# Early output projection by column halves over four tiles, in a two-layer encoder kernel

## The chip, the cores and the metric

The kernel runs on one core of one Trainium2 chip. The metric is the device time of the whole program in microseconds; the time before is the median of three runs. The profile shows one further execution.

## The reference

A two-layer encoder trunk over 1024 tokens of width 1024, all in float32. Each layer normalises its input, projects it with one wide matrix into several head groups and a gate, runs attention in the groups, multiplies the concatenated heads by SiLU(gate) and applies an output projection that is added to the residual. Cut to what matters here:

```python
def even_layer(x, mem_n, ...):                     # layer 0
    h = rmsnorm(x, norm_g)
    aq, ak, av, bq, bk, bv, xq, gate = _split(h @ w_in, EVEN_SPLITS)
    y_a = windowed_gqa_sink(...)                   # (A) 6 heads, band of 128
    y_b = dense_gqa_blocked(...)                   # (B) 6 heads, dense
    y_x = memory_cross_attention(xq, mem_n, ...)   # (X) 4 heads, 256 memory tokens
    y = concat([y_a, y_b, y_x]) * silu(gate)       # (1024, 1024)
    return x + y @ w_out

def odd_layer(x, mem_n, ...):                      # layer 1
    ...                                            # (C) 6 differential heads, and (X)
    y = concat([y_c, y_x]) * silu(gate)            # (1024, 1024)
    return x + y @ w_out

h = odd_layer(even_layer(x))
return rmsnorm(h, final_norm)
```

## The kernel before

**Products in three matmuls.** Each float32 operand is split into a high part, rounded to the matmul's format, and a low part, the rest. A product is high x high, high x low and low x high, so each 128 x 128 x 512 block of a product is three matmuls. Splitting is a cast on ScalarE (ACT) and a subtraction on VectorE (DVE) or GpSimd (POOL).

**Attention in steps with filling.** `run_steps` (L431) writes down the program of a layer's attention step by step. A step holds one block of 128 queries of a head (in group A 256 queries): scores and exponential (`s1`), a copy of the probabilities through a DMA (`word_copy` or `hop`, tile er), two or three steps later their transposes and splits (`s2`), then the product with v and the gating (`s3`). Layer 0 has 8 steps of X, 8 of the first B head and 64 of B and A mixed, numbered 0 to 79; layer 1 has 8 of X and 48 of C, 0 to 55. After the last step the loop runs four times more for the delayed parts.

Between the parts of a step the loop pulls work that does not depend on it, the filling. It comes from a list of jobs (`Jobs`, L88): first the input projections (`proj_jobs`, L277: 24 matmuls for 512 tokens of a 128-wide piece, tile acc), then the early output projection. One pull is eight matmuls, and `fill` says how many a step pulls, half of them ahead of the rest of the step and half at its end: 3 a step in X, in the first B head and in all of C, 1 in the rest of layer 0. A job whose condition is not met holds up those behind it in the list. The tile framework then places the program's instructions on the engines' queues, each of which runs in order, so in the trace pulled matmuls appear mixed with the attention's. All DMAs named here are issued by one queue, SyncE's (SP).

**The early output projection.** The concatenated, gated heads are stored in DRAM (`ysc`) as eight rows m of 128 channels, in the order in which they are finished (`KORD`); `stored` says which are there. `pre_job` (L645) takes one tile of 128 tokens, loads its first `EARLY[l]` rows (`y_chunk`, L613: DMAs into tile yr, then a split into yh and yl), and for each of the two column halves of the output multiplies them by w_out (`y_mm`, L632, tile pre), adds the residual (tile xh) and stores the sum in DRAM (`xpsc`). This is done for tiles 2 to 7 with five rows in layer 0 and for tiles 2 and 3 with seven rows in layer 1 (`PRE`, L42).

```python
when=lambda: len(wout) == 16 and all((l, m) in stored for m in range(EARLY[l]))
```

**w_out.** `load_wout` (L246) brings w_out in sixteen pieces of 128 x 512: pieces 0 to 7 are the rows of the first column half, 8 to 15 those of the second. The raw piece (tile wor) lands in a buffer of the wr kind (two) for the first half and of the wr, wh and wl kinds (two, four, four; the same as the weights and the y chunks use) for the second, is cast by ACT (woh), and its rest is taken by DVE for even pieces and POOL for odd ones (wol). The split pieces take the place of the layer's input hT, whose first half of tokens is free when the last projection job has come to its second half (`half`), and the second when that job is done. `wout_hook` (L258) is called once a step and issues up to `WRATE[l]` pieces, 3 in layer 0 and 4 in layer 1.

**The rest of the output projection.** `out_proj` (L1173) goes through the eight tiles in the order `ORD`. The first two begin with the rows below `EARLY[l]`, while the attention ends; then each tile gets the rows that are still missing (tile po), the residual or the stored partial sum, and the norm. In layer 0 the normalised tile is transposed into the input of layer 1 (`transpose_tile`).

Of the kernel before, what the change touches and what calls it, by code (L numbers as in the profile page):

```python
# [12 lines left out]
F32 = mybir.dt.float32  # L13
# [16 lines left out]
EARLY = (5, 7)  # L30
# [7 lines left out]
WRATE = (3, 4)  # L38
# [3 lines left out]
PRE = (range(2, 8), range(2, 4))  # L42
# [45 lines left out]
class Jobs:  # L88
# [25 lines left out]
    def _advance(self):  # L114
        if self.cur is None:
            i = self._next()
            if i is None:
                return False
            self._load(i)
            self.cur = (i, self.jobs[i]["run"](self.loaded[i]))  # L120
            self._load(i + 1)
        i, gen = self.cur
        try:
            next(gen)
        except StopIteration:
            self.done.update((self.jobs[i]["tag"],) + self.jobs[i].get("also", ()))
            self.loaded[i] = None
            self.cur = None
            return self._advance()
        return True  # L130

# [20 lines left out]
def encoder_kernel(ctx, tc, A):  # L152
# [93 lines left out]
    def load_wout(l, i, pl):  # L246
        nh, k = divmod(i, 8)
        if k == 0:
            wtile.append([pl.tile([P, 8, 512], F32R, tag="h", name="wo" + c, bufs=4) for c in "hl"])
        tag, bufs = (("wr", 2), ("wh", 4), ("wl", 4))[(0, 1, 2, 1, 2)[i % 5] if nh else 0]  # L250
        raw = wp.tile([P, 512], F32, tag=tag, name="wor", bufs=bufs)
        dma(raw, w_out[l][KORD[l][k], :, nh * 512:(nh + 1) * 512])
        hi, lo = (t[:, k, :] for t in wtile[nh])
        (nc.vector.tensor_copy if WHI[l] else nc.scalar.copy)(hi, raw)
        (nc.gpsimd if i % 2 else nc.vector).tensor_tensor(out=lo, in0=raw, in1=hi, op=ALU.subtract)
        return hi, lo

    def wout_hook(l, jobs, last, pl):  # L258
        lim = 16 if last in jobs.done else 8 if half[0] else 0
        for _ in range(WRATE[l]):  # L260
            if len(wout) < lim:
                wout[len(wout)] = load_wout(l, len(wout), pl)

    wout, wtile, half = {}, [], [False]

    def half_done():
        half[0] = True
# [9 lines left out]
    def proj_jobs(ws, hT, ntok, consumes, on_half=None):  # L277
        hh, hl = hT
        pend = []
        for c0, wi in ((c0, wi) for c0 in range(0, ntok, 512) for wi in range(len(ws))):  # L280
            if c0 > 0 and wi == 0 and on_half is not None:
                on_half()
# [148 lines left out]
    def run_steps(steps, jobs, hooks=None):  # L431
# [4 lines left out]
        for i in range(n + LAG + 1):  # L436
# [11 lines left out]
            if jobs is not None:  # L448
                jobs.pull(f - f // 2)
            for q in list(posts):  # L450
                q.pop(0)()
                if not q:
                    posts.remove(q)
# [14 lines left out]
            if jobs is not None:  # L468
                jobs.pull(f // 2)
        while posts:  # L470
            for q in list(posts):
                q.pop(0)()
                if not q:
                    posts.remove(q)
# [138 lines left out]
    def y_chunk(l, t, ks):  # L613
        ysv = ysc[l].rearrange("m p (t c) -> t p m c", c=P)
        out = {}
        for kh in range(2):
            for a, b in ((0, EARLY[l]), (EARLY[l], 8)):
# [3 lines left out]
                if (kh, 0) not in out:  # L621
                    out[kh, 0] = (wp.tile([P, 4, P], F32, tag="wr", name="yr", bufs=2),
                                  wp.tile([P, 4, P], F32R, tag="wh", name="yh", bufs=4),
                                  wp.tile([P, 4, P], F32R, tag="wl", name="yl", bufs=4))
                raw, hi, lo = out[kh, 0]
# [3 lines left out]
        return [(out[k // 4, 0][1][:, k % 4, :], out[k // 4, 0][2][:, k % 4, :]) if (k // 4, 0) in out else None  # L629
# [15 lines left out]
    def pre_job(l, t, src):  # L645
        rows = slice(t * P, (t + 1) * P)

        def run(ch):
            pend = []
            i = 0  # L650
            for nh in range(2):
# [4 lines left out]
                for k in range(EARLY[l]):  # L656
                    for _ in y_mm(acc, ch, nh, k, k == 0, k == EARLY[l] - 1):
                        i += 1
                        if i % 8 == 0:
                            yield  # L660
                nc.vector.tensor_tensor(out=xh, in0=acc, in1=xh, op=ALU.add)
                dma(xpsc[l][rows, cols], xh)
        return dict(tag="pre%d" % t, run=run, load=lambda: y_chunk(l, t, range(EARLY[l])),
                    when=lambda: len(wout) == 16 and all((l, m) in stored for m in range(EARLY[l])))

# [241 lines left out]
    for t in PRE[0]:  # L907
        jl.append(pre_job(0, t, x_d))
# [253 lines left out]
    def hooks0(i):  # L1162
        if 2 <= i < 8:
            skew(i - 2)
        wout_hook(0, jobs, "g2", r1)

    run_steps(steps, jobs, hooks0)
# [5 lines left out]
    def out_proj(l, hT_next, stack):  # L1173
# [6 lines left out]
        pre = [t for t in PRE[l] if "pre%d" % t in jobs.done]  # L1180
# [21 lines left out]
        def chunk(t):  # L1202
            return y_chunk(l, t, range(ne if t in pre else 0, 8))
# [5 lines left out]
        for i in range(2):  # L1209
            t = order[i]  # L1210
            accs[i] = pieces(i)
            if t not in pre:
                mm(accs[i][0], chs[i], range(ne), 0)
        xrs = [xres(t) for t in order[:2]]
        for i, t in enumerate(order):
            xr = xrs[i]
            mps, eps = accs[i] if i < 2 else pieces(i)
            mm(mps, chs[i], range(ne if i < 2 or t in pre else 0, 8), ne if t in pre else 0)
# [52 lines left out]
    half[0] = False  # L1271
# [69 lines left out]
    for t in PRE[1]:  # L1341
        jl.append(pre_job(1, t, x1sc))
# [119 lines left out]
    def hooks1(i):  # L1462
        wout_hook(1, jobs, "g5", r2)

    run_steps(steps, jobs, hooks1)
# [76 lines left out]
```

## Time and profile before

| | |
|---|---|
| median of 3 runs | 1274.36 us (1273.86 to 1276.91) |
| the profiled execution | 1277.62 us, span 1275.8 us |
| mean granted clock of TensorE | 0.986 |
| PE busy | 1218.1 us, 95% of the span |
| DVE, ACT, POOL busy | 850.7, 602.9, 426.6 us |
| matmuls of the early part (tile pre) | 264, started between 441.8 and 1190.4 us |

The times of the trace count from the start of the span. PE is TensorE's matmuls, PEld its weight loads, which run beside them. PEclk is the clock that TensorE was granted, as a part of full speed; a matmul at half the clock takes twice as long and counts as busy for that time, so a stretch can be full and still lose time. A row of the waits gives the waiting engine, tile and line, what ended the wait, the sum in us, the number of times and the longest.

### The profile page before, as it was taken

Reading aid. Unit: us, or ns where it says so; the run is one execution under the profiler, and the core shown is the slowest. Engines: PE = TensorE matmul, PEld = TensorE weight load, DVE = VectorE, ACT = ScalarE, POOL = GpSimd, SP = SyncE. Lnnn points to the kernel's source line nnn. Section 1 sums busy time; section 2 is a strip of 40 time slices with the busy share of each in tenths; the row PEclk is TensorE's granted clock in tenths of the full one; section 3 lists DMA queues with packets and bytes.
Section 4 is the critical chain, followed back from the end, with each engine's and each line's share of the span. In section 5 each row is a group of like instructions: output and inputs, shape, how many; then the busy total and the mean of one; then the engine's idle time right before and its main releaser. Section 6 shows DMA issues by size and latency. Waiting matters only on the chain.

```text
span 1275.8 us, 19602 instructions
## 1 busy us (share of the span) xinstructions
PE 1218.1 (95%) x6806; PEld 1008.8 (79%) x6806; DVE 850.7 (67%) x1623; ACT 602.9 (47%) x1275; POOL 426.6 (33%) x390
## 2 busy tenths in 40 slices
PE   6989989999999889999999999999999999999998
PEld 5878878888888678877888788787787877877886
DVE  5567676377778877748367866766767667577444
ACT  6245455266667755634134643444444444464222
POOL 5024255366666644413122212232222322231100
PEclk9999999999999889999999999999999999997999
DMA  6655334545465555467644424242332423353263
GB/s 248 195 183 162 123 146 156 176 157 203 149 223 199 201 191 192 164 184 244 192 138 149 149 91 131 83 139 100 133 121 83 140 99 129 119 199 125 89 215 117
DMA packets 95646, 198.85 MB, mean 156 GB/s; under 512 B 11286, under 2 KB 30998, under 8 KB 95548
## 3 DMA queue, kind: packets, MB, share of 16 engines
q1 hardware_dynamic: 95548, 197.60, 46.5%
q8 instruction: 54, 0.88, 0.3%
q14 instruction: 44, 0.36, 0.1%
HBM read 78.80 MB, written 30.95 MB: 86 GB/s over the span
## 4 chain that ended last, share of the span: by engine, by line
PE 46%; DVE 3%; issue 1%; ACT 1%; DMA 1%; POOL 0%; POOLq 0%; SPq 0%; DVEq 0%; ACTq 0%
PE acc L291 24%; PE po L636 5%; PE oc L1422 5%; PE sc L1383 3%; PE te L517 2%; PE sc L1389 2%; PE pre L636 2%; PE ox L593 1%; PE ssqc L1437 1%; DMA wor<-in_w_out 1%; PE tv L395 1%; PE sx L486 1%; DVE e L1407 1%; DVE mr L1405 0%; ACT e L568 0%
## 5 line engine op out<-in xcount | busy, mean ns | idle before, releaser
L291 PE MATMUL acc<-h,wh 128*128 128x512 f32 x1536 | 498.7, 399 | 5.7 <-DVE wh L235 2.1
L291 PEld LDWEIGHTS acc<-h,wh 128*128 128x128 f32 x1536 | 285.2, 189 | 73.7 <-issue 11.6
L291 PE MATMUL acc<-h,wl 128*128 128x512 f32 x768 | 304.8, 397 | 2.0 <-POOL wl L237 2.0
L237 POOL TENSOR_TENSOR wl<-wr,wh 128x512 fp32r<-128x512 f32 x96 | 124.2, 1295 | 334.4 <-DVE wh L235 132.8
L306 DVE TENSOR_TENSOR PTl<-te,PTh 128x512 fp32r<-128x512 f32 x224 | 146.4, 685 | 68.4 <-ACT PTh L305 67.5
L291 PEld LDWEIGHTS acc<-h,wl 128*128 128x128 f32 x768 | 145.0, 189 | 35.2 <-issue 4.4
L1398 ACT ACTIVATE e<-e,mn 128x1024 f32<-128x1024 f32 x96 | 110.2, 1150 | 111.4 <-DVE mn L1395 111.4
L305 ACT CAST PTh<-te 128x512 fp32r<-128x512 f32 x224 | 123.4, 592 | 64.2 <-PE te L517 56.1
L1395 DVE CUSTOM_DVE_ANT_0 e<-sc,toep 128x1024 f32<-128x1024 f32 x96 | 114.1, 1220 | 20.8 <-PE sc L1389 20.8
L1026 POOL TENSOR_TENSOR e<-e,rz 128x1024 f32<-128x1024 f32 x48 | 92.3, 1926 | 82.3 <-DVE rz L1025 62.7
L517 PEld LDWEIGHTS te<-identr,er 128*128 128x128 f32 x896 | 90.9, 143 | 14.7 <-issue 3.5
L517 PE MATMUL te<-identr,er 128*128 128x128 f32 x896 | 97.9, 247 | 4.0 <-issue 1.7
L1022 ACT ACTIVATE e<-sb,mr,nrq 128x1024 f32<-128x1024 f32 x48 | 58.0, 1209 | 48.6 <-DVE mr L1021 27.9
L235 DVE CAST wh<-wr 128x512 fp32r<-128x512 f32 x112 | 55.5, 498 | 30.9 <-PE acc L291 8.9
L1422 PE MATMUL oc<-PTh,v 128*128 128x256 f32 x384 | 74.9, 288 | 0.0
L636 PE MATMUL po<-woh,yh 128*128 128x512 f32 (+1 forms) x176 | 67.9, 387 | 0.1
L1454 POOL TENSOR_TENSOR gy<-O,gy 128x256 f32<-128x256 f32 x24 | 31.1, 1297 | 108.9 <-DVE O L1451 83.1
L636 PE MATMUL po<-woh,yl 128*128 128x512 f32 (+1 forms) x176 | 67.3, 382 | 0.0
L636 PE MATMUL po<-wol,yh 128*128 128x512 f32 (+1 forms) x176 | 67.2, 382 | 0.0
L1407 DVE SCALAR_TENSOR_TENSOR e<-e,mr 128x1024 f32<-128x1024 f32 x48 | 62.5, 1303 | 1.1
L1422 PEld LDWEIGHTS oc<-PTh,v 128*128 128x128 f32 x384 | 61.4, 191 | 0.7 <-ACT PTh L305 0.6
L1017 DVE TENSOR_REDUCE mn<-sb 128x1 f32<-128x1024 f32 x48 | 58.4, 1216 | 5.0 <-PE sb L486 4.9
(199 smaller groups left out, 2270.7 us busy)
## 6 DMA issues: line engine op xcount, KB each, us to landing
er<-e SPq DMA_DIRECT2D x112, 512.0 KB, 2.9
wr<-in_w_in SPq DMA_DIRECT2D x96, 256.0 KB, 2.7
ysc<-gy SPq DMA_DIRECT2D x16, 512.0 KB, 2.9
wor<-in_w_out SPq DMA_DIRECT2D x32, 256.0 KB, 3.5
cq<-sg SPq DMA_DIRECT2D x64, 128.0 KB, 2.4
ck<-sg SPq DMA_DIRECT2D x48, 128.0 KB, 2.3
er<-e SPq DMA_DIRECT2D x12, 384.0 KB, 3.0
xt<-in_x SPq DMA_DIRECT2D x8, 512.0 KB, 6.0
```

The lines of the kernel that those rows point to most:

```text
L237: (nc.vector if fast else nc.gpsimd).tensor_tensor(out=lo, in0=raw, in1=hi, op=ALU.subtract)
L291: lastmm[0] = nc.tensor.matmul(acc, a, b[:, k, c0:c0 + n], start=(i == 0), stop=(i == 23))
L305: nc.scalar.copy(hi, src)
L306: return nc.vector.tensor_tensor(out=lo, in0=src, in1=hi, op=ALU.subtract)
L517: nc.tensor.transpose(to[:, i * P:(i + 1) * P], e[0][:, k * P:(k + 1) * P], idt)
L636: lastmm[0] = nc.tensor.matmul(acc, a, b, start=(start and n == 0), stop=(stop and n == 2))
L1017: nc.vector.tensor_reduce(out=mn, in_=Sp, op=ALU.min, axis=AX.X)
L1026: nc.gpsimd.tensor_tensor(out=et, in0=et, in1=rz.to_broadcast([P, 1024]), op=ALU.mult)
L1395: nc.vector.tensor_tensor_reduce(out=et, in0=Sp, in1=toeps[h][:, w0:w0 + 1024], scale=1.0, scalar=BIG, op0=ALU.add, op1=ALU.min, accum_out ...
L1398: nc.scalar.activation(et, et, AF.Exp, bias=mn[:, m:m + 1], scale=-1.0, accum_out=z[:, m:m + 1])
L1407: nc.vector.scalar_tensor_tensor(out=es[0], in0=es[1], scalar=c, in1=es[0], op0=ALU.mult, op1=ALU.add)
L1422: nc.tensor.matmul(acc, V[:, kt, v, :], pt[:, kt, :], start=(n == 0), stop=(n == 23))
```

## The change

- **Jobs.** The early part is now a list of groups with their number of rows. Layer 0: tiles 2, 3, 4 and 5 with four rows, tile 6 with six, tile 7 with six. Layer 1: tiles 2 and 3 with six, tile 4 with six. A group of several tiles is two jobs, one for each column half over all its tiles; a single tile stays one job for both halves.
- **Conditions.** A job of the first half asks for eight w_out pieces and the group's rows; the others for sixteen.
- **Chunks.** The chunks of y are loaded one ahead of their use and kept over both halves; the first two are asked for while the last projection job is still running (`half` is 2 then). `CUTS` says where a chunk's loads are divided, so that each part can be loaded by itself.
- **w_out.** The hook that issues the pieces is called after each of the two portions of a step's filling, with 1 piece in layer 0 and 2 in layer 1. Odd pieces land in a buffer of the sg kind (three in layer 0, five in layer 1, also used by xh), even ones in wr.
- **Pace.** Once all projections are done and eight pieces are issued, the filling of a step is set by `pace`: in layer 0 one pull in three steps of four, none in the fourth, in layer 1 two.
- **out_proj** takes for each tile the rows that its early part left out. Tiles 0 and 1 begin with six rows in layer 0 (before: five) and seven in layer 1.

```diff
-EARLY = (5, 7)
+EARLY = (6, 7)
+CUTS = ((0, 4, 6, 8), (0, 4, 6, 7, 8))
-WRATE = (3, 4)
+WRATE = (1, 2)
-PRE = (range(2, 8), range(2, 4))
+PRE = ((((2, 3, 4, 5), 4), ((6,), 6), ((7,), 6)), (((2, 3), 6), ((4,), 6)))
...
+    def projected(self):
+        return all("load" in j or j["tag"] in self.done for j in self.jobs)
...
-        tag, bufs = (("wr", 2), ("wh", 4), ("wl", 4))[(0, 1, 2, 1, 2)[i % 5] if nh else 0]
-        raw = wp.tile([P, 512], F32, tag=tag, name="wor", bufs=bufs)
+        raw = sg(M, "wor", F32) if i % 2 else wp.tile([P, 512], F32, tag="wr", name="wor", bufs=2)
...
     def wout_hook(l, jobs, last, pl):
         lim = 16 if last in jobs.done else 8 if half[0] else 0
+        if half[0] == 2 and len(wout) >= 8 and len(chunks) < 2:
+            pre_chunk(l, len(chunks))
         for _ in range(WRATE[l]):
...
-            if c0 > 0 and wi == 0 and on_half is not None:
-                on_half()
+            if c0 > 0 and on_half is not None:
+                on_half(wi + 1)
...
-    def run_steps(steps, jobs, hooks=None):
+    def run_steps(steps, jobs, hooks=None, pace=None):
...
             if jobs is not None:
+                if half[0] and len(wout) >= 8 and jobs.projected():
+                    f = pace(i)
                 jobs.pull(f - f // 2)
+                if hooks:
+                    hooks(-1)
...
                 jobs.pull(f // 2)
+                if hooks:
+                    hooks(-1)
...
-            for a, b in ((0, EARLY[l]), (EARLY[l], 8)):
+            for a, b in zip(CUTS[l], CUTS[l][1:]):
...
+    def pre_chunk(l, n):
+        order = [(t, k) for ts, k in PRE[l] for t in ts]
+        if n < len(order):
+            t, k = order[n]
+            if t not in chunks and all((l, m) in stored for m in range(k)):
+                chunks[t] = y_chunk(l, t, range(k))
+
+    def pre_jobs(l, src):
+        out = []
+        for ts, k in PRE[l]:
+            parts = [(0,), (1,)] if len(ts) > 1 else [(0, 1)]
+            for nhs in parts:
+                out.append(dict(
+                    tag="pre%s%d" % (ts[0], nhs[0]), also=tuple("pre%d" % t for t in ts) if nhs[-1] else (),
+                    run=lambda _, ts=ts, k=k, nhs=nhs: pre_run(l, ts, k, nhs, src), load=lambda: None,
+                    when=lambda k=k, nhs=nhs: len(wout) >= 8 * nhs[-1] + 8 and all((l, m) in stored for m in range(k))))
+        return out
+
+    def pre_run(l, ts, kn, nhs, src):
+        order = [t for tt, _ in PRE[l] for t in tt]
+        i = 0
+        for nh in nhs:
+            for t in ts:
+                n = order.index(t)
+                pre_chunk(l, n)
...
                 acc = ps_a("pre")
-                for k in range(EARLY[l]):
-                    for _ in y_mm(acc, ch, nh, k, k == 0, k == EARLY[l] - 1):
+                for k in range(kn):
+                    for _ in y_mm(acc, chunks[t], nh, k, k == 0, k == kn - 1):
                         i += 1
                         if i % 8 == 0:
                             yield
+                    if k == 0 and (t != ts[-1] if nh == 0 else t == ts[-1]):
+                        pre_chunk(l, n + 1)
...
     def hooks0(i):
         if 2 <= i < 8:
             skew(i - 2)
-        wout_hook(0, jobs, "g2", r1)
-
-    run_steps(steps, jobs, hooks0)
+        if i < 0:
+            wout_hook(0, jobs, "g2", r1)
+
+    run_steps(steps, jobs, hooks0, lambda i: i % 4 != 3)
...
-        pre = [t for t in PRE[l] if "pre%d" % t in jobs.done]
+        pre = {t: k for ts, k in PRE[l] for t in ts if "pre%d" % t in jobs.done}
...
-            return y_chunk(l, t, range(ne if t in pre else 0, 8))
+            return y_chunk(l, t, range(pre.get(t, 0), 8))
...
-            if t not in pre:
-                mm(accs[i][0], chs[i], range(ne), 0)
+            mm(accs[i][0], chs[i], range(pre.get(t, 0), ne), pre.get(t, 0))
...
-            mm(mps, chs[i], range(ne if i < 2 or t in pre else 0, 8), ne if t in pre else 0)
+            mm(mps, chs[i], range(ne if i < 2 else pre.get(t, 0), 8), pre.get(t, 0))
...
     def hooks1(i):
-        wout_hook(1, jobs, "g5", r2)
-
-    run_steps(steps, jobs, hooks1)
+        if i < 0:
+            wout_hook(1, jobs, "g5", r2)
+
+    run_steps(steps, jobs, hooks1, lambda i: 2)
```

More of the change, by code (lines that the diff above doesn't have):

```diff
@@ L262, in wout_hook, with half_done @@
                 wout[len(wout)] = load_wout(l, len(wout), pl)
-    wout, wtile, half = {}, [], [False]
-    def half_done():
-        half[0] = True
+    wout, wtile, half = {}, [], [0]
+    chunks = {}
+    def half_done(n=1):
+        half[0] = n
     lastmm = [None]
@@ L620, in y_chunk @@
                     continue
[L621 to L625, printed above, removed]
+                if kh not in out:
+                    out[kh] = (wp.tile([P, 4, P], F32, tag="wr", name="yr", bufs=2),
+                               wp.tile([P, 4, P], F32R, tag="wh", name="yh", bufs=4),
+                               wp.tile([P, 4, P], F32R, tag="wl", name="yl", bufs=4))
+                raw, hi, lo = out[kh]
                 o = slice(a - 4 * kh, b - 4 * kh)
@@ L628, in y_chunk @@
                 split_to(hi[:, o, :], lo[:, o, :], raw[:, o, :], 0.5)
-        return [(out[k // 4, 0][1][:, k % 4, :], out[k // 4, 0][2][:, k % 4, :]) if (k // 4, 0) in out else None
+        return [(out[k // 4][1][:, k % 4, :], out[k // 4][2][:, k % 4, :]) if k // 4 in out else None
                 for k in range(8)]
@@ L643, in store_y @@
         stored.add((l, m))
[L645 to L651, printed above, removed]
+    def pre_chunk(l, n):
[21 more added lines that the diff above has]
+                pre_chunk(l, n)
+                rows = slice(t * P, (t + 1) * P)
                 cols = slice(nh * 512, nh * 512 + 512)
@@ L660, in run @@
                             yield
+                    if k == 0 and (t != ts[-1] if nh == 0 else t == ts[-1]):
+                        pre_chunk(l, n + 1)
                 nc.vector.tensor_tensor(out=xh, in0=acc, in1=xh, op=ALU.add)
                 dma(xpsc[l][rows, cols], xh)
-        return dict(tag="pre%d" % t, run=run, load=lambda: y_chunk(l, t, range(EARLY[l])),
-                    when=lambda: len(wout) == 16 and all((l, m) in stored for m in range(EARLY[l])))
     left = ExitStack()
@@ L906, in encoder_kernel @@
     jl.sort(key=lambda j: JORD.index(j["tag"]))
-    for t in PRE[0]:
-        jl.append(pre_job(0, t, x_d))
+    jl.extend(pre_jobs(0, x_d))
     jobs = Jobs(jl, ld)
@@ L1270, in encoder_kernel @@
     wtile.clear()
-    half[0] = False
+    half[0] = 0
+    chunks.clear()
     hT = hT1
@@ L1340, in encoder_kernel @@
     jl[-1]["also"] = ("g5",)
-    for t in PRE[1]:
-        jl.append(pre_job(1, t, x1sc))
+    jl.extend(pre_jobs(1, x1sc))
     jobs = Jobs(jl, ld)
```

## The prediction

> **What bounds the kernel now.** I read the page's busy shares and clock strip first, then busy time by stretch around the stages the change touches, then the waits of PE there, then single instructions.
>
> ```profile
> PE 1218.1 (95%) x6806; PEld 1008.8 (79%) x6806; DVE 850.7 (67%) x1623; ACT 602.9 (47%) x1275; POOL 426.6 (33%) x390
> ...
> PEclk9999999999999889999999999999999999997999
> ```
> PE is busy 95% of the span, no other engine over 67%, and the strip shows the granted clock below full in two places: slices 14 and 15 (415 to 478 us) and slice 37 (1148 to 1180). PE's 5% of idle time and those clock losses are all that can be won without removing matmuls. By stretch (length, then busy time of PE, PEld, DVE, ACT and POOL, then the clock):
>
> ```profile
> 423.00:442.00 19.00, 15.66 (x88) 12.76 (x87) 18.19 (x31) 14.91 (x35) 15.56 (x11) 0.82 0.35 134
> 442.00:552.00 110.00, 104.80 (x627) 89.11 (x627) 80.88 (x179) 61.39 (x144) 50.06 (x48) 0.97 0.50 179
> ...
> 1142.00:1156.00 14.00, 10.39 (x61) 7.56 (x61) 13.04 (x23) 12.23 (x24) 7.97 (x7) 0.95 0.44 157
> 1156.00:1195.00 39.00, 39.00 (x194) 31.44 (x193) 23.92 (x46) 14.48 (x30) 3.25 (x4) 0.84 0.36 122
> ```
> From 423 to 442 PE is idle for 19.00 - 15.66 = 3.3 us and its clock averages 0.82, a loss of 19 x 0.18 = 3.4 us; from 442 to 552 the clock costs 110 x 0.03 = 3.3 us. In layer 1 the same pair stands at 1142 to 1156 (3.6 us idle, 14 x 0.05 = 0.7 of clock) and 1156 to 1195 (no idle, 39 x 0.16 = 6.2 of clock). In the idle stretches DVE is nearly saturated: 18.19 of 19 and 13.04 of 14.
>
> ```profile
> 423.17 0.39 PE L291 MATMUL acc<-h,wl 128*128 128x512 f32 x1
> ...
> 441.83 0.46 PE L636 MATMUL pre<-woh,yh 128*128 128x512 f32 x1
> ...
> 1141.23 0.39 PE L291 MATMUL acc<-h,wl 128*128 128x512 f32 x1
> ...
> 1155.93 0.63 PE L636 MATMUL pre<-woh,yh 128*128 128x512 f32 x1
> ```
> Why there: the last projection matmul (acc) of layer 0 is at 423.17 and the first early output matmul (pre) at 441.83; in layer 1 it is 1141.23 and 1155.93. Between them PE has attention work alone. By the program this is the stretch in which the filling has run out: counting pulls step by step, layer 0's last gate ends in step 56, and pre2 may start only in step 60, when the sixteenth w_out piece is issued (the fifth head pair is stored in step 56). In layer 1 the last gate ends in step 51, and pre2 starts in step 53, for both its sixteen pieces and the seventh row (stored in step 52).
>
> ```profile
> PE pre L636 <- DVE yt L428: 3.7, 1, 3.7
> PE te L517 <- issue: 1.7, 1, 1.7
> PE sa L486 <- ACT e L1022: 1.7, 1, 1.7
> PE te L517 <- DVE PTa L306: 0.8, 1, 0.8
> ...
> PE sc L1383 <- DVE mn L1395: 2.2, 2, 1.5
> PE rbcc L1449 <- DVE PTl L306: 1.4, 1, 1.4
> PE tv L395 <- DVE PTl L306: 1.1, 1, 1.1
> ```
> The waits of PE, first 395 to 470 us, then 1110 to 1170: single waits of 3.7, 1.7 and 0.8 us in layer 0 and 1.1 to 1.5 in layer 1, all on DVE, ACT or a late transfer (issue).
>
> ```profile
> 430.50:432.00 1.50, 1.14 (x9) 0.68 (x7) 1.50 (x4) 1.05 (x3) 1.50 (x3) 1.00 0.98 399
> ...
> 432.00:433.50 1.50, 0.13 (x1) 0.13 (x2) 1.44 (x3) 1.48 (x3) 1.50 (x1) 1.00 0.02 5
> ...
> 435.00:436.50 1.50, 1.32 (x7) 1.25 (x8) 1.50 (x5) 1.50 (x4) 1.17 (x1) 0.50 0.01 3
> ...
> 450.00:451.50 1.50, 0.00 (x0) 0.00 (x0) 1.50 (x2) 0.00 (x0) 1.50 (x1) 0.97 0.62 238
> 451.50:453.00 1.50, 0.58 (x1) 0.50 (x2) 1.44 (x3) 0.00 (x0) 0.75 (x2) 0.50 0.92 260
> ...
> 1152.50:1154.00 1.50, 0.94 (x6) 0.43 (x4) 1.50 (x4) 1.50 (x5) 0.61 (x1) 1.00 0.05 19
> ...
> 1155.50:1157.00 1.50, 1.50 (x6) 1.20 (x5) 1.50 (x3) 0.64 (x2) 0.00 (x0) 0.50 0.06 20
> ```
> The clock does not need one long gap to fall: 432.0 to 433.5 had 0.13 of 1.5 busy and the clock was at 0.50 by 435; 1152.5 to 1154 had 0.94 and it was at 0.50 by 1155.5. The second fall in layer 0 follows the 3.7 us wait (nothing busy in 450.0 to 451.5).
>
> The Trainium skill, "TensorE: Matmul & The Clock Gate", section "HAM oscillation — how this bites in real kernels", puts the limit at PE-idle gaps of about 3.4 us. The trace disagrees in two of the three falls: their longest single waits are 1.7 and 1.5 us. By that rule the change, which leaves no gap so long, would give back all 13.6 us of clock, and the time would be 1257.7 instead of the 1259.3 below.
>
> **The change part by part.** *Matmuls.* Layer 0's early part shrinks from 6 tiles x 5 x 2 x 3 = 180 matmuls to 96 + 36 + 36 = 168, layer 1's grows from 84 to 72 + 36 = 108; out_proj does the rest, so PE's total is unchanged: 0 us. What moves is when they can start. With four stored rows and eight pieces as the condition for the first column half, layer 0's early part starts in step 57, right behind the last gate, and its 21 pulls run to step 82 because three steps in four get one. In layer 1 it starts in step 51 and its 13.5 pulls, two a step, last to step 57, past the last score step.
>
> ```profile
> 1205.29 17.28 PE po L636 x76
> ...
> L661 DVE TENSOR_TENSOR xh<-pre,xh 128x512 f32<-128x512 f32 x16 | 11.0, 686 | 1.7 <-PE pre L636 1.6
> ...
> L255 DVE TENSOR_TENSOR wol<-wor,woh 128x512 fp32r<-128x512 f32 x16 | 15.6, 988 | 3.0 <-ACT woh L254 3.0
> ...
> SPq L171 <- DMA xpsc<-xh: 11.7, 7, 2.5
> ```
> A pull is eight matmuls of 17.28/76 = 0.227 us, 1.8 us. In layer 0 steps 57 to 59 get two pulls, 3.6 us of PE work into 3.3 us of idle. But DVE was saturated there and keeps its w_out halves (0.99 us each, eight a layer), now with an xh addition (0.69) beside it, so the steps also stretch. I take two thirds of the idle back, 2.2 us (bounds 0 and 3.3), and all 3.4 of the clock (0 and 3.4), since two filled steps in three lift the windows that had almost nothing.
>
> *The 3.7 us wait.*
> ```profile
> 448.29 3.62 DVE L309 SCALAR_TENSOR_TENSOR yl<-yr,yh 128x512 fp32r<-128x512 f32 x2 [0.36 <-ACT yh L308]
> ...
> 447.57 4.19 POOL L1026 TENSOR_TENSOR e<-e,rz 128x1024 f32<-128x1024 f32 x2
> ...
> L309 DVE SCALAR_TENSOR_TENSOR yl<-yr,yh x48: 264/554/1975, 443.5 to 1251.4; 128x512 fp32r<-128x512 f32 x16, 128x128 fp32r<-128x128 f32 x16, 128x384 fp32r<-128x384 f32 x16
> ```
> PE waited for an accumulator bank that DVE should have freed, and DVE spent 3.62 us on two yl splits (median 0.55, longest 1.98) while POOL ran two multiplications. The burst was pre3's chunk, two pieces at once. The new chunks of tiles 2 to 5 are one piece each, two loaded ahead while the gates run, so the pair is gone; a single stretched split is not. I take back half of 3.7 + 3.3 = 7.0, so 3.5 (bounds 0 and 7.0).
>
> The Trainium skill, "SBUF — State Buffer", section "SBUF: two separate sides", says that a DVE instruction with two SBUF inputs and a GpSimd one that reads SBUF exclude each other for the whole instruction. The row agrees (3.62 us of splits beside 4.19 us of POOL), and this speaks against the change: it does not take either instruction away.
>
> *w_out's pieces.*
> ```profile
> 1124.07 6.63 SPq L171 DMA_DIRECT2D wor<-in_w_out  x8
> ...
> 1133.09 0.62 ACT L254 CAST woh<-wor 128x512 fp32r<-128x512 f32 x1 [2.98 <-DMA wor<-in_w_out]
> ...
> 1140.23 0.62 ACT L254 CAST woh<-wor 128x512 fp32r<-128x512 f32 x1 [2.48 <-DMA wor<-in_w_out]
> ```
> In layer 1 eight transfers went out in 6.63 us, and ACT stood 2.98 and 2.48 us in front of casts whose piece had not landed, with the exponentials queued behind. Now two pieces go with each pull portion: still four a step in layer 1, two instead of three in layer 0. The odd pieces land in sg buffers instead of the wr, wh and wl ones. Casts (0.6 us on ACT) and subtractions are the same number. In layer 1, steps 51 and 52 get three and two pulls where they had two and none. With DVE still the limit in those steps I take back two thirds of 3.6, 2.4 (bounds 0 and 3.6); the 6.9 us of clock I take whole (bounds 0 and 6.9), since no step there is left without at least two pulls. The 1.1 us wait at the transpose of v lies before the gap and stays.
>
> *What the new buffers cost.* In layer 0 sg has three buffers, and xh holds one from its load until its xpsc store lands. SP waited on such a store 7 times, 11.7 us, 1.7 each; a DMA that waits there holds up the copy er<-e of the next step behind it. Four odd pieces fall into the steps with xh: at most 4 x 1.7 = 6.8 us, 0 if PE has filling meanwhile; one late copy cost PE 1.7 us (the issue row), and I charge one: 1.7. The w_out pieces moved between the portions pass the er copies on SP in the same way; that is in this bound.
>
> *Out_proj.*
> ```profile
> L1253 DVE SCALAR_TENSOR_TENSOR xs<-x,r,gb 128x1024 f32<-128x1024 f32 x14 | 18.0, 1285 | 9.4 <-POOL r L225 9.4
> L1232 DVE TENSOR_TENSOR x<-po,xr 128x1024 f32<-128x1024 f32 x14 | 17.1, 1221 | 12.1 <-PE po L636 12.1
> ...
> L306 DVE TENSOR_TENSOR h<-tx,h 128x512 fp32r<-128x512 f32 x16 | 10.4, 685 | 1.4 <-ACT h L305 1.4
> ...
> L309 DVE SCALAR_TENSOR_TENSOR yl<-yr,yh 128x384 fp32r<-128x384 f32 x16 | 8.7, 554 | 17.4 <-ACT yh L308 17.4
> ...
> 600.19 1.06 PE L334 MATMUL tx<-ident,xs 128*128 128x128 f32 x8
> ...
> 1195.00:1276.00 81.00, 74.11 (x367) 61.28 (x365) 32.21 (x55) 19.08 (x43) 7.79 (x12) 0.99 0.44 146
> ```
> In layer 0 tiles 6 and 7 keep 12 matmuls each (before 18), tiles 2 to 5 get 24. A light tile has 12 x 0.227 + 1.1 of transposes = 3.8 us on PE, but DVE needs 1.28 + 1.22 + 2 x 0.69 + about 0.55 = 4.4 and small ones, 4.6: the last two tiles lag by 2 x 0.8 = 1.6 us, in front of layer 1's first projection. I charge 1.6 (bounds 0, if the first half of the projections covers it, and 1.6). In layer 1 each tile's chunk comes in four pieces instead of three, 8 more transfers, casts and splits (at most 8 x 0.55 = 4.4 us on DVE), hidden while DVE is busy 32.21 of 81 us; without that cover it costs the 4.4. The third early tile adds two xh loads, additions (0.69 each) and stores to a stretch where DVE has 23.92 of 39; their cost is 0 there, and 1.4 without the cover. Tiles 0 and 1 starting with six rows instead of five reorders work, 0 us.
>
> *Sum.* Gains 2.2 + 3.4 + 3.5 + 2.4 + 6.9 = 18.4, costs 1.7 + 1.6 = 3.3, net 15.1 us. The profiled execution took 1277.62 us (span 1275.8), so it would take 1262.5. It lies 3.26 us above the median of the runs, 1274.36, and I carry the difference over: **1259.3 us**. With every gain at its bound (24.2) and no cost it is 1250.2.
>
> **The rivals.**
> *More comes back.* Every gain at its bound: about 1250. For it: PE has work ready in every idle place. Against: DVE's 18.19 of 19.
>
> *The split blocks again.* The 3.7 us wait and its clock recur, and a second like it: the half of 7.0 that I took is lost, then 7.0 more: 1269.8. For it: both instructions remain, and a longest split of 1.98. Against: one such pair in 48 splits.
>
> *Layer 0 returns nothing.* With fewer pulls the later steps are held by DVE and the chain behind er<-e, not by PE, and what the gap gains is waited away later: only layer 1's 9.3 less 3.3 of costs remain, 1268.4. For it: DVE is at 80.88 of 110 there already and the steps would be shorter. Against: PE at 104.80 of 110.
>
> *It doesn't do what it says.* The attention queues are still stopped by w_out's casts and DVE's halves, four pieces a step in layer 1, and pulled matmuls only change places: about 1274, no change.
>
> *Slower: the unfilled fourth step.* Steps 59, 63, 67, 71, 75 and 79 get no pull. If each drops the clock as the gap did (3.4 us a fall), six cost 20.4 and the time is 1279.7; it decides from the fifth on (4.4 falls eat the 15.1). For it: the falls came after stretches of short waits. Against: in the gap three steps in a row were unfilled while DVE also had w_out's halves.
>
> **How the numbers follow.** My forecast has a chance of 0.38, with its own range of 1253 to 1266; more comes back 0.12, layer 0 returns nothing 0.18, the split blocks again 0.12, nothing done 0.12, slower 0.08. The range that leaves out no more than 2 in 10 is 1249 to 1272: it cuts most of the last two. A measurement can tell about 0.3%, 3.8 us, from no change, so faster means below 1270.5. The first four cases lie there, the two at 1268 to 1270 narrowly: 0.74 faster, 0.17 the same, 0.09 slower.
>
> **What would show it.** Right: pre starts within 3 us of the last acc in both layers; the clock stays at 1.00 from 425 to 475 and in layer 1's last 100 us; PE is idle under 3 us in the stretches that answer to those above; no 3 us wait in front of pre. Wrong: clock falls spread over layer 0's last 25 steps (the fourth step); SP waiting for xpsc stores with er<-e behind them (sg); idle PE in front of tx at out_proj's end over 3.6 us (light tiles); or early matmuls started on time with the stage no shorter (DVE).

## The result, and the profile after

| | before | after |
|---|---|---|
| median (lowest to highest) | 1277.47 us, 8 runs (1271.67 to 1281.96) | 1267.36 us, 8 runs (1263.64 to 1270.35) |
| ratio after / before | | 0.9929, 95% interval 0.991 to 0.9949 |
| the profiled execution | 1277.62 us, span 1275.8 | 1265.36 us, span 1263.6 |

The change is 0.7% faster: by the interval 6.5 to 11.5 us, where the prediction said 15.1. The mechanism works, but some 40% of the forecast gain is missing. Of the 8.1 us between 1259.3 and 1267.36, 3.1 belong to the kernel before, whose median is 1277.47 over eight runs and was 1274.36 over the first three. The two profiled executions lie 12.3 us apart, more than the runs, so the profiles flatter the change a little; the sum had put the second at 1262.5, and it took 1265.36. One of the nine runs of e7 below took 1875.93 us at a clock of 0.565; its ratio and clock leave that run out.

First the page of the changed kernel, busy shares and the clock strip:

```profile
PE 1207.2 (96%) x6806; PEld 1001.5 (79%) x6806; DVE 848.8 (67%) x1633; ACT 603.9 (48%) x1283; POOL 423.5 (34%) x390
...
PEclk9999999999999999999999999999999999999999
```
The same 6806 matmuls are busy 10.9 us less (1218.1 before), and 8.4 of that is clock (busy time times what the clock lacks to 1, taken in windows of 1 us: 16.1 before, 7.7 after). The dents in slices 14, 15 and 37 are gone from the strip, where a 9 stands for 0.90 or more, so that short falls do not show.

The stretches that answer to the four of before (layer 0's attention after the last projection, in two parts, and layer 1's; after the times come the length, busy time of PE, PEld, DVE, ACT, POOL, and the clock):

```profile
425.00:444.00 19.00, 16.79 (x101) 14.36 (x99) 15.34 (x31) 14.21 (x32) 12.02 (x10) 0.91 0.63 217
444.00:537.00 93.00, 90.49 (x573) 76.69 (x572) 74.90 (x170) 59.87 (x137) 51.62 (x50) 1.00 0.56 201
...
1137.00:1151.00 14.00, 12.33 (x79) 9.98 (x77) 11.00 (x21) 10.62 (x23) 7.10 (x6) 1.00 0.68 226
1151.00:1190.00 39.00, 39.00 (x238) 32.61 (x237) 30.14 (x58) 17.95 (x37) 4.66 (x6) 1.00 0.43 148
```
Layer 1 is as predicted: idle falls from 3.6 to 1.7 us and no clock is lost. In layer 0 the idle time of the first stretch falls from 3.3 to 2.2, but the clock still averages 0.91 there.

Single matmuls of the changed kernel, the last acc and the first pre of each layer:

```profile
425.18 0.39 PE L297 MATMUL acc<-h,wl 128*128 128x512 f32 x1
...
428.83 0.40 PE L648 MATMUL pre<-woh,yh 128*128 128x512 f32 x1
...
1137.07 0.39 PE L297 MATMUL acc<-h,wl 128*128 128x512 f32 x1
1138.55 0.46 PE L648 MATMUL pre<-woh,yh 128*128 128x512 f32 x1
```
The early part now begins 3.7 and 1.5 us behind the last projection, before 18.7 and 14.7.

PE's waits from 395 to 470 us, then from 1110 to 1170, and the SP queue's for partial sums over the whole span (sum, times, longest):

```profile
PE sa L498 <- ACT e L1052: 2.0, 2, 1.1
PE te L529 <- issue: 1.7, 2, 1.3
PE pre L648 <- DVE yt L434: 1.2, 1, 1.2
...
PE pre L648 <- ACT sqc L1457: 1.7, 1, 1.7
...
SPq L175 <- DMA xpsc<-xh: 7.4, 6, 2.0
```
The 3.7 us wait in front of pre is now 1.2, and SP waits for xpsc stores less than before (11.7 us then).

Whole stages of the kernel before: layer 0's attention from 400 to its last oa or ob, layer 0's last po to layer 1's first score (sc), and layer 1's last 30 us of projections to its last oc:

```profile
400.00:550.74 150.74, 139.98 (x833) 118.33 (x831) 117.41 (x243) 92.06 (x209) 80.42 (x72) 0.95 0.53 188
599.85:704.45 104.60, 98.76 (x550) 84.14 (x549) 60.79 (x121) 35.44 (x108) 23.13 (x22) 0.98 0.53 158
1111.23:1202.08 90.85, 86.09 (x469) 68.77 (x469) 60.19 (x107) 45.13 (x87) 19.07 (x19) 0.92 0.39 137
```
The same stages after the change:

```profile
400.00:537.04 137.04, 129.61 (x796) 109.53 (x795) 111.69 (x238) 90.75 (x203) 78.36 (x71) 0.98 0.57 204
593.23:701.54 108.31, 100.28 (x550) 84.87 (x549) 63.12 (x122) 35.58 (x109) 23.58 (x24) 0.97 0.52 156
1107.07:1190.55 83.48, 81.81 (x491) 67.47 (x490) 62.81 (x114) 45.79 (x91) 19.90 (x19) 1.00 0.48 161
```
Idle plus clock (both added up from windows of 1 us, the clock as above) falls by 6.2 us in the first, from 10.77 + 6.08 to 7.42 + 3.23; in the third by 9.7, from 4.75 + 6.59 to 1.67 + 0.00; and the second gives 3.3 back, from 5.84 + 1.63 to 8.03 + 2.71. So layer 0 returned two thirds of what it should, layer 1 all, and the start of layer 1, where 1.6 was charged, took twice that.

A further cost stands behind layer 1's last oc, where PE waits once (changed kernel, 1190.55 to the end):

```profile
PE po L648 <- DVE x L1262: 1.5, 1, 1.5
```
All fourteen profiled executions with the new layer 1, those of the experiments below among them, have this wait, and PE's idle time there is 8.0 to 8.7 us; the three with the old layer 1 do not have it and are idle for 6.7. Tile 4 now comes third with two rows left and tile 2 fourth with two, and PE stands before the next tile until DVE has added up tile 4, whose accumulator it needs. No run takes this wait away.

### The profile page after: what moved, and what is told of

The parts are those of the page before. It is cut to its first block, busy times and chain, and to the rows that moved or that the text cites. A ratio compares the mean times of both kernels' runs of the same rounds, so it can differ in the third digit from the quotient of the medians.

```text
span 1263.6 us, 19629 instructions
## 1 busy us (share of the span) xinstructions
PE 1207.2 (96%) x6806; PEld 1001.5 (79%) x6806; DVE 848.8 (67%) x1633; ACT 603.9 (48%) x1283; POOL 423.5 (34%) x390
## 4 chain that ended last, share of the span: by engine, by line
PE 48%; DVE 3%; issue 1%; ACT 1%; POOL 0%; DMA 0%; POOLq 0%; SPq 0%; DVEq 0%; ACTq 0%
PE acc L297 25%; PE oc L1452 5%; PE po L648 4%; PE sc L1413 3%; PE te L529 3%; PE sc L1419 2%; PE pre L648 2%; PE ox L605 1%; PE tv L401 1%; PE ssqc L1467 1%; PE sx L498 0%; PE rbcc L1479 0%; DVE xs L1283 0%; ACT e L580 0%; DVE e L1437 0%
```

## The experiments

Medians of five rounds. Ratios are to runs of the kernel before on the same chip, with the 95% interval; kernels of different jobs are compared by their ratios. Clock is the mean granted clock over the runs (e11: the median, as one of its runs lists 0.948).

| kernel | median us | ratio | clock |
|---|---|---|---|
| e1 layer 0 alone | 1271.73 | 0.9965 (0.9945 to 0.9984) | 0.990 |
| e2 layer 1 alone | 1269.06 | 0.994 (0.9919 to 0.996) | 0.989 |
| e3 late conditions | 1276.19 | 1.001 (0.9989 to 1.003) | 0.986 |
| e4 a pull in every step | 1267.52 | 0.9922 (0.9904 to 0.9941) | 0.991 |
| e5 first half in wr only | 1267.43 | 0.9936 (0.9917 to 0.9955) | 0.993 |
| e6 all wol on DVE | 1262.95 | 0.9905 (0.9884 to 0.9927) | 0.993 |
| e7 four sg buffers | 1270.64 | 0.995 (0.9932 to 0.9968) | 0.991 |
| e8 light tiles third and fourth, by tile order | 1262.66 | 0.99 (0.9881 to 0.992) | 0.995 |
| e9 the change again | 1265.44 | 0.9919 (0.9897 to 0.9942) | 0.993 |
| e10 light tiles third and fourth, by choice of tiles | 1259.24 | 0.9876 (0.9851 to 0.9901) | 0.995 |
| e11 e8 with e6 | 1255.63 | 0.9848 (0.9822 to 0.9875) | 0.996 |
| e12 before, all wol on DVE | 1272.45 | 0.9979 (0.996 to 0.9999) | 0.989 |
| e13 xh loaded late | 1266.53 | 0.9935 (0.9912 to 0.9957) | 0.992 |
| e14 e10 with e6 | 1257.07 | 0.9857 (0.9836 to 0.9879) | 0.995 |
| e15 e14 with e13 | 1258.93 | 0.987 (0.9848 to 0.9892) | 0.994 |

**Which layer (e1, e2).** One layer of the kernel is that of the change, the other has the old conditions, buffers and hooks, in short:

```diff
-CUTS = ((0, 4, 6, 8), (0, 4, 6, 7, 8))
+CUTS = ((0, 4, 6, 8), (0, 7, 8))            # e1: layer 1 as before
...
+CUTS = ((0, 5, 8), (0, 4, 6, 7, 8))         # e2: layer 0 as before
```


> The change in layer 0 alone, layer 1 as before. Theory (layer 0 returned 6.2 us in attention and the stretch behind it gave 3.7 back): 2 to 3 us faster than before, ratio about 0.998, with the clock fall at 405 to 415 and the one at 435 to 445 as in the changed kernel and layer 1's two late falls as before. Rival (layer 0's early part is worth the 9.1 us forecast, and layer 1's change took some away): ratio about 0.993. Rival (layer 0 returns nothing): 1.000, the early matmuls only changing places.

> The change in layer 1 alone, layer 0 as before. Theory: 9 to 10 us faster than before, ratio about 0.9925, so all of the net gain is layer 1's; the stretch from layer 0's last po to layer 1's first sc as long as before (104.6 us). Rival (layer 1's gain needs layer 0's other order): under 5 us, ratio over 0.996.

Measured: 0.35% and 0.6%, that is 4.5 us (2 to 7) and 7.7 us (5 to 10), together 12, which is the whole within these intervals. Layer 0 does return something. The 9.1 us forecast for its attention did not all reach the end: 0.993 lies outside e1's interval. But less the two charges of 3.3, both in layer 0, the forecast was 5.8, or 0.9955, and that lies inside, as layer 1's 9.3 does. So these two runs do not say which layer fell short; the profiles do. In e1's profile the fall at 412 came and the one at 435 did not, and layer 1's late falls are there from 1156.5 to 1170.2. In e2 the stretch from layer 0's last po to layer 1's first sc is 103.17 us.

**Is it the earlier start (e3)?**

```diff
-when=lambda k=k, nhs=nhs: len(wout) >= 8 * nhs[-1] + 8 and all((l, m) in stored for m in range(k))
+when=lambda k=k, nhs=nhs: len(wout) == 16 and all((l, m) in stored for m in range((5, 7)[l]))
```


> The changed kernel, but its early output-projection jobs wait, as before, for all 16 pieces of w_out and for five (layer 0) or seven (layer 1) stored rows; the column halves, the buffers, the paced filling and the places of the pieces are those of the changed kernel. Theory (the earlier start is what returns time): the first pre comes over 10 us behind the last acc again in both layers, both gaps reopen with their clock falls, and the time is 8 to 14 us over the changed kernel's. Rival (what counts is how w_out's pieces are spread, not when the early part starts): within 4 us of the changed kernel.

Measured: no gain at all over the kernel before. The column halves, the buffers and the new places of the pieces bring nothing without the earlier conditions. One point failed: layer 1's first pre came only 3.3 us behind the last acc (1142.29, 1145.57), not over 10; there the time was lost at the other end, with pre still running at 1201.93, past the last oc at 1196.37. In layer 0 it was both: first pre 19.9 us late, the last at 542.17, past the last ob at 536.51. So an early part that starts late also ends too late for the attention to cover.

**Is it the fourth step (e4)?**

```diff
-    run_steps(steps, jobs, hooks0, lambda i: i % 4 != 3)
+    run_steps(steps, jobs, hooks0, lambda i: 1)
```


> The changed kernel with a pull in every step of layer 0, also in the fourth. Theory (the unfilled fourth steps cost nothing: the clock stands at 1.00 there): no gain; the early part runs out five to six steps sooner, and the last steps stand idle: 0 to 4 us slower than the changed kernel. Rival (the fourth step's emptiness is what layer 0's shortfall of 2.9 us went to): 2 to 3 us faster than the changed kernel.

Measured: the time of the changed kernel (0.9922 beside 0.9929 and 0.9919), although the early part ended 14 us sooner (last pre at 522.70, not 536.34). The unfilled fourth steps neither cost the missing time nor save any.

**The light tiles (e8, e10).** Two edits with the same aim. The first changes the order of tiles, the second keeps the order and gives tiles 2 and 3 the six rows:

```diff
-ORD = ((0, 1, 2, 3, 4, 5, 6, 7), ...)
+ORD = ((0, 1, 6, 7, 2, 3, 4, 5), ...)                               # e8
...
-PRE = ((((2, 3, 4, 5), 4), ((6,), 6), ((7,), 6)), ...)
+PRE = ((((4, 5, 6, 7), 4), ((2,), 6), ((3,), 6)), ...)              # e10
```


> The changed kernel with layer 0's tiles of the output projection in the order 0, 1, 6, 7, 2, 3, 4, 5, so that the two light tiles (12 matmuls each) are not last. Theory (DVE lags behind light tiles, and this is in front of layer 1's first projections): PE idle from layer 0's last oa to layer 1's first acc falls by 1 to 2 us, and the time by 1 to 3 us. Rival (the time given back at layer 1's start is its transfers', not the light tiles'): no change within 1 us.

> The changed kernel, but the four tiles with four early rows are 4 to 7 and the two with six are 2 and 3; the output projection still goes through the tiles in the order 0 to 7, so its two light tiles come third and fourth and not last. Theory (light tiles at the end leave PE waiting for DVE and put layer 1's start out of order): 3 to 5 us faster than the changed kernel, as with the other order of tiles. Rival (the other order of tiles helped by storing x1's tiles in another order for layer 1): within 1.5 us of the changed kernel.

Measured: 0.990 and 0.9876. On one chip e10 is 6.2 us under the changed kernel (e9), more than the 3 to 5 expected. As the second edit leaves the order of x1's tiles alone, it is the place of the light tiles that counts. The stretch from layer 0's last po to layer 1's first sc in e8:

```profile
594.92:697.18 102.26, 97.07 (x550) 83.02 (x549) 60.04 (x119) 35.20 (x108) 23.09 (x22) 1.00 0.52 159
```
and in e10:

```profile
592.88:694.55 101.67, 96.99 (x550) 82.99 (x549) 60.12 (x119) 35.06 (x108) 23.07 (x22) 1.00 0.51 160
```
With the same 550 matmul rows it is 6.0 and 6.6 us shorter than after the change, and 2.3 and 2.9 shorter than before, with the clock at 1.00. PE's waits in that region (575 to 705), changed kernel:

```profile
PE tx L340 <- DVE h L312: 1.7, 1, 1.7
PE sx L498 <- DMA xkh<-sg: 1.3, 2, 0.9
...
PE acc L297 <- DVE v L1271: 1.2, 1, 1.2
```
In e10 the three are gone, and the largest of those left is one that was 0.7 in the changed kernel:

```profile
PE tx L340 <- DVE xs L1283: 1.6, 2, 1.2
```
The wait for v and h is DVE's lag behind the light tiles. The one for xkh is a consequence of the order that was built with them: the first cross-attention score (sx) stands at 626.8 instead of 647.9 before and 638.2 in e10, ahead of its transferred keys, and the clock fell behind it.

All seventeen profiled executions divide the same way. In the nine with the light tiles last the stretch takes 107.9 to 109.3 us, sx stands 33.6 to 34.2 us behind the last po, and some clock is lost in every one. In the five with them third and fourth it takes 101.7 to 103.2 us, sx stands 45.3 to 46.1 us behind, and no clock is lost. In the three with layer 0's old early part it takes 103.2 to 104.6 us, sx stands 46.7 to 48.1 us behind, and two of the three lose clock.

**POOL's subtractions (e6, e11, e14, e12).**

```diff
-        (nc.gpsimd if i % 2 else nc.vector).tensor_tensor(out=lo, in0=raw, in1=hi, op=ALU.subtract)
+        nc.vector.tensor_tensor(out=lo, in0=raw, in1=hi, op=ALU.subtract)
```
Two engines of the changed kernel around 400 us:

```profile
399.89 3.78 POOL L258 TENSOR_TENSOR wol<-wor,woh 128x512 fp32r<-128x512 f32 x3
...
400.59 3.63 DVE L258 TENSOR_TENSOR wol<-wor,woh 128x512 fp32r<-128x512 f32 x1
...
405.67 0.45 PE L498 MATMUL sa<-ak,q 128*128 128x384 f32 x1 [0.99 <-ACT e L1052]
...
407.64 0.72 PE L529 MATMUL te<-identr,er 128*128 128x128 f32 x4 [1.34 <-issue]
```
One subtraction on DVE (0.69 us as a rule) lasts as long as three on POOL beside it; the exponential behind it on ACT waits, and PE with it.

> The changed kernel with all of w_out's subtractions (wol) on DVE, none on POOL. Theory (DVE's stretched 3.63 us subtraction is POOL's 3.78 us ones beside it): no wol on DVE over 1.5 us in layer 0 and no waits at 400 to 410; but DVE has 16 more subtractions of about 0.7 us, 8 to a layer, in stretches where it sets the pace: net between 2 us faster and 3 us slower than the changed kernel. Rival (the stretch has another cause): a subtraction of over 3 us on DVE again.

> Both: layer 0's tiles in the order 0, 1, 6, 7, 2, 3, 4, 5, and all of w_out's subtractions on DVE. Theory (two separate losses, 4.5 us at the end of the output projection and 3.9 us of splits held up by POOL): they add, 7 to 9 us under the changed kernel, ratio to before 0.985 to 0.988. Rival (both only remove the same random falls of the clock): 4 to 5 us under the changed kernel, ratio about 0.9895.

> Tiles 2 and 3 as the light ones, and all of w_out's subtractions on DVE. Theory (two separate losses that add): 1.5 to 4 us faster than with the swap alone, ratio to before 0.984 to 0.987. Rival (both remove the same falls): ratio 0.9875 again.

> The kernel before, with all of w_out's subtractions on DVE. Theory (POOL's halves cost time because the changed kernel lets five pieces land at once): no gain, ratio 0.998 to 1.003, since DVE is the busiest engine around w_out's pieces. Rival (POOL's 1.3 us subtractions hold up DVE's splits and exponentials' sums wherever they stand): 2 to 4 us faster, ratio about 0.9975.

Durations of wol (least, median, longest, ns), changed kernel:

```profile
L258 DVE TENSOR_TENSOR wol<-wor,woh x16: 677/690/3631, 396.4 to 1156.1; 128x512 fp32r<-128x512 f32 x16
```
and e6:

```profile
L258 DVE TENSOR_TENSOR wol<-wor,woh x32: 668/686/1502, 398.6 to 1154.0; 128x512 fp32r<-128x512 f32 x32
```
DVE has 16 subtractions more and yet the kernel is faster, by 2 to 3 us in e6, 6.6 from e8 to e11, 2.4 from e10 to e14 (ratios times 1275). Only the second is clear of its two intervals, but all go one way. The subtractions of over 3 us are gone. The first and third stage in e6:

```profile
400.00:536.21 136.21, 128.41 (x804) 108.42 (x802) 117.65 (x250) 93.48 (x209) 70.75 (x66) 1.00 0.59 208
...
1105.83:1187.28 81.45, 81.45 (x492) 67.53 (x490) 66.44 (x122) 46.55 (x91) 9.50 (x11) 1.00 0.49 165
```
No clock is lost in layer 0's attention in any of the four changed kernels with this edit (e6, e11, e14, e15); the ten other profiles with the new layer 0 lost 1.5 to 4.7 us there. In layer 1's stage the idle time is at most 0.3 us in the four, where the changed kernel has 1.67 and 1.33 (e9). DVE is busier (117.65 of 136, before the edit 111.69 of 137) and is not what limits. In e12 the edit helps the kernel before too, 2.7 us (0.1 to 5): my theory that only the change makes POOL's halves costly fell. The longest subtraction on DVE was 2.10 us before, so the loss was there; the change made one of 3.6.

**Bunching and late pieces (e5, e7, e13).** My first reading of the fall at 405 was that five pieces of w_out land at once, and of the one at 435 that the second half lands late for want of sg buffers.

```diff
-raw = sg(M, "wor", F32) if i % 2 else ...
+raw = sg(M, "wor", F32) if i % 2 and nh else ...         # e5
...
-sg=3        +sg=4                                         # e7, layer 0
...
-                xh = sg(M, "xh", F32)
-                dma(xh, src[rows, cols])
                 acc = ps_a("pre")
                 for k in range(kn):
+                    if k == kn - 1:
+                        xh = sg(M, "xh", F32)
+                        dma(xh, src[rows, cols])          # e13
```


> The changed kernel, but the raw pieces of w_out's first half land in the two wr buffers only, not in sg ones too. Theory (five pieces landing at once put five casts in a row on ACT and a 3.6 us subtraction on DVE at 400, which cost PE 2.3 us of waits and about 1.7 of clock): the fall at 405 to 415 is gone and the time is 2 to 3 us under the changed kernel's. Rival (with two buffers the first half is ready later and the early part starts late): the first pre 5 us or more behind the last acc, and no gain or a loss of up to 5 us.

> The changed kernel with four sg buffers instead of three in layer 0. Theory (the second half's pieces come late because two of the three sg buffers hold prefetched xh): w_out's second half is transferred earlier, the cast's 3.4 us wait for its piece at 433 shrinks, the clock fall at 435 to 445 with it: 2 to 3 us under the changed kernel. Rival (the first half then bunches more, six pieces at once): the fall at 405 to 415 is deeper, and no gain.

> The changed kernel, but each early job takes its sg buffer for the residual (xh) and loads it only before the last of its rows instead of before the first. Theory (w_out's second half lands late because prefetched xh hold two of layer 0's three sg buffers, and this is the wait at 433 with the fall at 435 to 445): the cast that waited 3.4 us for its piece waits under 1.5 us, the fall there is gone, 1.5 to 3 us faster than the changed kernel. Rival (the second half is late because ACT and DVE are full at 400 to 430, not for want of a buffer): a dip at the same place and no gain over 1 us; or the later xh makes the additions wait, 1 to 3 us slower.

> All three edits: light tiles 2 and 3, the subtractions on DVE, xh loaded late. Theory: 1 to 3 us under the kernel with the first two, ratio about 0.983. Rival (once DVE's splits are not held up, the late pieces cost nothing): the same time within 1 us.

None is faster than the change (0.9936, 0.995, 0.9935; e15 0.987 beside e14's 0.9857). In e5 the fall at 405 is gone as expected, but layer 0's attention is no shorter (its last oa or ob comes at 537.47, in the changed kernel at 537.04): PE stands idle at 420 to 425 and 430 to 435 instead, and the clock falls later:

```profile
405.00:410.00 5.00, 4.57 (x25) 3.32 (x24) 4.97 (x10) 4.23 (x9) 3.10 (x3) 1.00 0.78 274
...
420.00:425.00 5.00, 3.50 (x22) 2.91 (x22) 4.55 (x11) 3.23 (x8) 1.46 (x3) 1.00 0.54 184
430.00:435.00 5.00, 3.59 (x25) 2.89 (x23) 3.60 (x6) 2.95 (x6) 2.81 (x4) 1.00 0.83 290
435.00:440.00 5.00, 4.07 (x18) 3.21 (x19) 4.94 (x9) 3.72 (x6) 3.73 (x3) 0.72 0.54 200
```
In layer 1, where the edit also holds, the rival came: the first pre stands 5.9 us behind the last acc (1137.03, 1142.89), and the stage that answers to the 83.48 us above takes 86.58 us at a clock of 0.96. So e5 cannot price the bunching in layer 0 by its time.

In e7 the rival came: the clock was 0.50 from 410 to 415, and the longest subtraction on DVE took 4.90 us. In e13 the late piece came hardly sooner; its cast in the changed kernel,

```profile
433.49 0.62 ACT L257 CAST woh<-wor 128x512 fp32r<-128x512 f32 x1 [3.40 <-DMA wor<-in_w_out]
```
and in e13:

```profile
431.92 0.62 ACT L257 CAST woh<-wor 128x512 fp32r<-128x512 f32 x1 [2.80 <-DMA wor<-in_w_out]
```
So the profiles do not show that the places at which the pieces land were what layer 0 lost, and the theory of held buffers fell. What makes the second half late I did not settle; with the subtractions on DVE it cost no clock.

**How much is chance (e9).**

> The changed kernel once more, beside a second set of runs of the kernel before, to see how much of one profiled execution is chance. Theory (the falls of the clock come in some executions and not in others, so the 1.7, 3.2 and 2.7 us of the first profile are one draw): the ratio is again 0.991 to 0.995, and the idle time of each stage repeats within 1 us while the clock's losses at 180, 405, 435 and 630 differ by 1 us or more. Rival (the falls belong to the schedule): the same losses at the same places.

The same kernel in two executions, 180 to 190 us, first the one profiled after the change:

```profile
180.00:190.00 10.00, 7.88 (x38) 6.39 (x37) 8.14 (x16) 4.41 (x10) 7.49 (x6) 0.83 0.59 225
```
then e9:

```profile
180.00:190.00 10.00, 7.94 (x48) 6.70 (x47) 9.03 (x16) 5.80 (x13) 7.48 (x7) 1.00 0.63 235
```
The same wait of 2.1 us (for yt, on DVE) brought the clock to 0.83 in one and left it at 1.00 in the other. The idle time of the stages repeats within 2.2 us (the start 26.09 and 23.96, the others within 0.8), the clock's losses differ: start to 400 us 1.71 and 2.96, layer 0's attention 3.23 and 1.71, start of layer 1 2.71 and 1.65. Of the named falls those at 435 and 630 came in both executions, those at 180 and 405 in one only, so theory and rival are each half right. In all seventeen profiled executions the first 400 us, which the edits hardly touch, cost 1.6 to 8.5 us of clock.

## Why the prediction was too high

*Right.* Where the time was lost and why: the early part's late start (e3). Layer 1's 2.4 + 6.9 = 9.3, measured 9.7 in the profile and 5 to 10 in e2. The 3.7 us wait became 1.2. The fourth step cost nothing, and idle time fell under 3 us in both stretches. SP's xpsc waits shrank, so nothing of the 1.7 charged for the sg buffers shows; that the costs still come to 3.3 in the profiles, as in the sum, is luck, because the light tiles took it all. By the signs I had named: pre within 3 us of the last acc held in layer 1 (1.5) and was missed in layer 0 (3.7); the clock held 1.00 in layer 1 and not in layer 0 (0.91 from 425 to 444).

*The term that failed first: out_proj's light tiles.* I charged 1.6, as DVE's lag of 2 x 0.8 us, and put 1.6 as the upper bound. The pair of profiles shows 3.3 us of idle time and clock in that stretch, and over all profiles it averages 108.5 us with the light tiles last, beside 104.0 with the old layer 0: 4.5 us. Taking them from the end was worth 6.2 us (e10 beside e9, ratios 0.9876 and 0.9919: 5.5). The lag on DVE was real; the bound was wrong because it ended at the tile. Layer 1's first projections wait for those tiles, the built order then puts the first score ahead of its keys, and the clock fell there. With the light tiles third and fourth the stretch averages 102.3 us, 1.7 less than with the old layer 0. Its idle time is alike (4.7 to 6.2 us, and 5.3 to 5.9), so this rest is mostly clock, lost in two of those three executions.

A term put at nothing belongs here: layer 1's output projection, where I called the added cost hidden because DVE is busy 32.21 of 81 us. The wait for x costs 1.5 us there. A mean share of busy time does not show a row of light tiles: the first four in the order have 6, 6, 12 and 12 matmuls left.

*The second: layer 0's clock.* I took 2.2 of idle time, 3.4 of clock, and 3.5 for the wait and the fall behind it, 9.1 in all; the profile shows 6.2. The idle time came back nearly as forecast (3.3 of 4.05), the clock did not (2.8 of 5.05). The rival "the split blocks again" described what did happen, in another place: not the yl pair at 448, but w_out's own halves on DVE and POOL at 400, one of 3.63 us where the longest before was 2.10. I had kept these subtractions at "the same number" and priced them at nothing; without POOL's the same kernel wins 2 to 7 us. The long subtraction explains the fall at 405; the one at 435 is gone in all four kernels with the edit too, but why is not shown. The Trainium skill, "SBUF — State Buffer", section "SBUF: two separate sides", says that a DVE instruction with two SBUF inputs and a GpSimd one that reads SBUF lock each other out for whole instructions; the trace agrees (3.63 us beside 3.78), and moving POOL's part away removed it.

*The third: falls of the clock taken as gone for good.* Over the 65 runs beside the experiments the kernel before has a mean clock of 0.9862 and 1275.7 us, the changed one over 14 runs 0.9921 and 1266.5 us. At some 1210 us of busy PE the clock accounts for 1210 x 0.0059 = 7.1 of the 9.2 us, idle time and the rest for 2.1. I had forecast 3.4 + 1.65 + 6.9 = 12.0 of clock and 3.1 of the rest. So most of what is missing is clock. The one execution of before is not to blame for the total, since its clock, 0.986, is that of the 65 runs. What failed is counting each of its falls as gone: of the 8.4 us of clock in the pair of profiles, layer 1 gave 6.6 of 6.9, layer 0's attention 2.8 of 5.05, and the start of layer 1 lost 1.1 more than before. The Trainium skill's rule in "TensorE: Matmul & The Clock Gate", section "HAM oscillation — how this bites in real kernels", an idle gap of about 3.4 us, would have given 1257.7; the traces go against it again, with the clock at 0.74 from 405 to 410 behind waits of 0.99 and 1.34 us.

## What to carry to other kernels

When work is taken out of a stage early, look at which tiles are left light and where they stand: third and fourth they cost almost nothing in layer 0 and 1.5 us in layer 1, where the tiles ahead of them have less left, and at the end they exposed the slower engine and moved the next stage's start. Do not take a fall of the clock as gone for good because its cause is: it can come at another place, or in one execution and not in the next. A pair of engines that share an elementwise job can hold each other up; it may be faster to give all of it to the busier one. With both corrections the kernel takes 1255.63 us (e11), 0.9848 of before.

## What I had not expected of the hardware

The clock is partly chance. Beside the two executions at 180 us, e11 had a stretch with 2.77 us busy of 5 (waits of 1.46 and 0.77 us) and no fall:

```profile
625.00:630.00 5.00, 2.77 (x12) 1.66 (x11) 0.43 (x1) 0.00 (x0) 1.27 (x1) 1.00 0.46 137
```
Taking 1210 x (1 - clock) off each run, the spread (standard deviation) of the kernel before falls from 2.7 to 1.6 us over 65 runs: most of what differs from run to run is the granted clock. A listed clock can also be wrong: one run of e11 lists 0.948 and took 1255.69 us, like the others.
